# FFN up products on x times norm weight with the root applied behind, five tall sets in each FFN, and one pool of weight tiles for the whole kernel

## The chip, the cores and the metric

The kernel runs on one core of a Trainium2 chip. The metric is the device time of one execution in microseconds (us). Before the change the median of three runs is 1173.68 us (1173.27 to 1174.42). The engines are TensorE (PE: matmuls; PEld: its weight loads), VectorE (DVE), ScalarE (ACT), GpSimd (POOL) and SyncE (SP). Each takes its instructions strictly in the order in which they stand in its own queue. SP and POOL also issue DMA transfers.

## The reference

One block of a language model in float32, with 512 tokens and model width 1024: an FFN, a mixer (a short convolution and a gated linear attention) and a second FFN, each on a normalised input and each added to the residual.

```python
def rmsnorm(x, g):
    y = x * lax.rsqrt(jnp.mean(x * x, axis=-1, keepdims=True) + EPS)
    return y * g
def swiglu(x, w_gu, w_down):
    g, u = jnp.split(x @ w_gu, 2, axis=-1)          # w_gu: 1024 x 5632
    return (jax.nn.silu(g) * u) @ w_down            # w_down: 2816 x 1024
...
x = x + 0.5 * swiglu(rmsnorm(x, norm_ffn1_g), ffn1_w_gu, ffn1_w_down)
x = x + hybrid_mixer(rmsnorm(x, norm_mix_g), w_in, ...)
x = x + 0.5 * swiglu(rmsnorm(x, norm_ffn2_g), ffn2_w_gu, ffn2_w_down)
return rmsnorm(x, final_norm_g)
```

## The kernel before

**Tiles.** x lies transposed: eight tiles `x[k]` of 128 features by 512 tokens. Every float32 product is made of three matmuls in the reduced type fp32r: each operand is split in a high part (a cast) and a low part (the rest), and the product is high times high, high times low, low times high. A weight tile `f` of 128x1024 (512 KB) comes by a DMA on SP's queue; ScalarE casts it into `wh` (line 393) and VectorE subtracts that into `wl` (394). There are three buffers of `wh` and three of `wl`, so a step's cast waits until TensorE has finished the step three before it; the method `take` of the class `Weights` issues the split of a step two steps ahead.

**Three ways of multiplying.** *Plain*: `mm_group` and `mm_single` multiply one 128-column block of weights at a time, with the weights as the stationary operand and x's 512 tokens moving: 24 matmuls of 512 columns for one block of 128 outputs. *Tall* (`Tall.run`) and *set* (`Set.run`) use a Strassen-like scheme: seven products, named m1, p2, q6, p5, q7, p3 and p4, in place of eight. A tall covers four blocks of gate columns and four of up columns with 168 matmuls of 512 columns, has x as the stationary operand, and so gives its result with the tokens on the partitions; `turn` transposes it back (32 transposes of 128x128 for a tall). A set covers two blocks of each with 168 matmuls of 256 columns, with no transposes. The seven operands made of x (class `Operands`, tiles `op`, lines 676 and 677) are sums of quarters of the normalised x, kept in the last eight tiles of `hid`; those made of the weights are sums that POOL makes with adding DMAs (line 362) and VectorE.

**The FFN's up products before.** The 22 pairs of blocks are four plain (two in `mm_group`, which is started while x still comes in, and two in `mm_single`), four talls and one set. The plain ones use `Norm`: x times the norm weight, split as it is (lines 496 to 500), and the root of the mean square as a row `row` that multiplies the outputs on VectorE (`plain_pair`). The sum of squares over the features is two matmuls with a matrix of ones (529, 530). The talls and the set use x times norm weight times row (`normed`, line 757).

**Order.** TensorE's order in the talls and sets is program order (`manual_schedule`); elsewhere a scheduler sets the order of each engine when the kernel is built, and the chip keeps to it. The pools of `hid`, `tp` and `f` belong to a phase (first FFN, mixer, second FFN) and are opened anew in each.

Of the kernel before, what the change touches and what calls it, by code (L numbers as in the profile page):

```python
# [103 lines left out]
PLAIN1, PLAIN2 = 4, 4  # L104
# [27 lines left out]
TALL_ORDER = ("m1", "p2", "q6", "p5", "q7", "p3", "p4")  # L132
TALL = {}


def tall(name, mat, cols, base=0):
# [6 lines left out]
    STEPS.extend((n, p) for p in TALL_ORDER for n in firsts)  # L143

# [13 lines left out]
def up_plan(up, plain, slow):  # L158

    kinds = ["tall"] * ((KF - plain) // 4)  # L160
    kinds.insert(len(kinds) if slow else 1, "set")
    f = plain
    for kind in kinds:
        if kind == "tall":
            tall((up, f), up, (f * P, DFF + f * P))
# [11 lines left out]
def ffn_plan(up, down, plain, slow):  # L177

    units(group(up, KD, (0, DFF, P, DFF + P), slow))
    for f in range(2, plain):  # L180
        units(single(up, KD, f * P))
        units(single(up, KD, DFF + f * P))
    up_plan(up, plain, slow)
# [32 lines left out]
ffn_plan("ffn1_w_gu", "ffn1_w_down", PLAIN1, True)  # L216
mixer_plan()
ffn_plan("ffn2_w_gu", "ffn2_w_down", PLAIN2, False)
# [8 lines left out]
def block_kernel(ctx: ExitStack, tc: tile.TileContext, xT, vecs, gf, gup, wgl, wts, out):  # L227
# [76 lines left out]
    for n, b in (("wh", 3), ("wl", 3), ("op", 14)):  # L304
        pools[n] = ctx.enter_context(tc.tile_pool(name=n, bufs=b))
    acc_row = ctx.enter_context(tc.tile_pool(name="acc_row", bufs=1))
    class Weights:
# [15 lines left out]
        def phase(self, early, first=6):  # L323
# [4 lines left out]
            for i in range(lo, self.end):  # L328
                n, p = STEPS[i]
                if p == "m1" and n in TALL:  # L330
                    self.loads.setdefault(i - (4, 3)[TALL[n][1]], []).append(n)
                    self.firsts.setdefault(i - (1, 0)[TALL[n][1]], []).append(n)
# [31 lines left out]
        def issue(self):  # L364
            at = self.issued
            self.fetch(at)
            for n in self.loads.get(at, ()):
                self.raw[n] = [self.dma(n + i) for i in range(4)]
# [144 lines left out]

    def rstd_rows(accs, width):
# [47 lines left out]
    class Set:  # L562
# [8 lines left out]

        def run(self, p):
            b = {"m1": "b", "p2": "a", "q6": "b", "p5": "c", "q7": "b", "p4": "b", "p3": "c"}[p]
            if self.group.joint:
                return self.run_joint(p, b)
# [6 lines left out]
            for k in range(4):  # L582
                for e in range(2):
                    s = slice(k * HW + e * P, k * HW + (e + 1) * P)
                    t = slice(k * HW, (k + 1) * HW)
                    to = o[:, e * HW : (e + 1) * HW]
                    for j, (ww, aa) in enumerate(((h, bh), (h, bl), (l, bh))):
# [9 lines left out]
        def run_joint(self, p, b):  # L597
            fresh = b not in self.bank
            two_banks = b != "b"
            if fresh:  # L600
                self.bank[b] = MM2() if two_banks else MM()
            o = self.bank[b]
            parts = self.group.get(p)
            h, l = W.take()
            for k in range(4):
                a = parts[k // 2][:, (k % 2) * S : (k % 2 + 1) * S]
                for e in range(2):
                    s = slice(k * HW + e * P, k * HW + (e + 1) * P)
                    if two_banks:
                        nc.tensor.matmul(o[:, e], h[:, s], a, start=fresh and k == 0,  # L610
                                         stop=False, skip_group_check=True)
                        nc.tensor.matmul(o[:, e, HW:], l[:, s], a[:, :HW], start=False,
                                         stop=k == 3, skip_group_check=True)
                        continue
                    to = o[:, e * HW : (e + 1) * HW]
                    for j, (ww, aa) in enumerate(((h, a[:, :HW]), (h, a[:, HW:]),
                                                  (l, a[:, :HW]))):
                        nc.tensor.matmul(to, ww[:, s], aa, start=fresh and k == 0 and e == 0 and j == 0,
                                         stop=k == 3 and j == 2, skip_group_check=True)
            if p in self.keep:  # L620
                v = T()
                nc.scalar.copy(v, o)
                self.v[p] = v
            self.done(self, p)

    class Operands:
# [5 lines left out]
        def __init__(self, b, joint=False):  # L632
            self.b = b
            self.joint = joint
            self.parts = {}
            self.sums = set()
# [20 lines left out]
        def make(self, p):  # L657
            if p in self.parts:
                return
            i = self.ORDER.index(p)  # L660
            if i > 0:
                self.make(self.ORDER[i - 1])
            v = self.sum(p)
            if self.joint:
                t = [tile_of("op", [P, 1024], F32R) for _ in range(2)]
                for i in range(2):
                    a = t[i].rearrange("p (k b t) -> p k b t", b=2, t=HW)
                    vi = v[:, 2 * i : 2 * i + 2]
                    nc.scalar.copy(a[:, :, 0], vi)
                    nc.vector.tensor_tensor(out=a[:, :, 1], in0=vi,  # L670
                                            in1=a[:, :, 0].bitcast(F32), op=ALU.subtract)
                self.parts[p] = t
                return
# [61 lines left out]
    def ffn(up, down, norm, nxt, plain, at):  # L735
        xh, xl = norm.h, norm.l
        rows = []

        def finish(k):
            if k == at:  # L740
                rows.append(norm.finish())

        o = mm_group(up, KD, (0, DFF, P, DFF + P), xh, xl, extra=finish, slow=nxt is not None)
        row = rows[0]
        hid = tile_of("hid", [P, KF, S])
        xn = {}

        def normed(j, l):


            if (j, l) not in xn:
                t = slice(l * HW, (l + 1) * HW)
                f = KF - KD + 4 * j
                v = hid[:, f : f + 4, t]
                for i in range(4):
                    k = 4 * j + i
                    nc.vector.scalar_tensor_tensor(
                        out=v[:, i], in0=x[k][:, t],
                        scalar=vec[:, norm.goff + k : norm.goff + k + 1], in1=row[:, t],
                        op0=ALU.mult, op1=ALU.mult)  # L760
                xn[j, l] = v
            return xn[j, l]

        xo = Operands(normed)

        def plain_pair(f, g, u):
            s, t = T(), T()
            mul(s, g, row)
            nc.scalar.activation(s, s, AF.Silu)
            mul(t, u, row)  # L770
            mul(hid[:, f], s, t)

        xo.make("m1")
        plain_pair(0, o[0], o[1])
        xo.make("p2")
        plain_pair(1, o[2], o[3])
        for f in range(2, plain):
            g = mm_single(up, KD, f * P, xh, xl)
            u = mm_single(up, KD, DFF + f * P, xh, xl)
            if f == 2:  # L780
                xo.make("p5")
            if f == 3:
                xo.sum("q6")
            plain_pair(f, g, u)
# [3 lines left out]
        def up_tall(f):  # L788
            g, u = {}, {}

            def done(p, banks):
                for t in range(2):
# [16 lines left out]
                    if p == "p3":  # L809
                        nc.vector.tensor_tensor(out=g[2 + t], in0=b, in1=g[2 + t], op=ALU.add)  # L810
                        nc.scalar.activation(g[2 + t], g[2 + t], AF.Silu)
                        mul(u[t], u[t], g[2 + t])
                    if p == "p4":
                        nc.vector.scalar_tensor_tensor(out=g[t], in0=b, scalar=-1.0, in1=g[t],
                                                       op0=ALU.mult, op1=ALU.mult)
# [13 lines left out]

        def up_set(i):  # L830
            f = [f for kind, f in UPS[up] if kind == "set"][i]
            h = hid[:, f : f + 2]

            def done(s, p):
                bank, v = s.bank, s.v
                if p == "p2":
                    s.g1 = T()
                    nc.vector.tensor_tensor(out=s.g1, in0=bank["a"], in1=v["m1"], op=ALU.add)
                    nc.scalar.activation(s.g1, s.g1, AF.Silu)
# [4 lines left out]
                if p == "p4":  # L844
                    nc.vector.scalar_tensor_tensor(
                        out=h[:, :, :HW], in0=pair(bank["b"]), scalar=-1.0, in1=pair(s.g1),
                        op0=ALU.mult, op1=ALU.mult)
                if p == "p3":
                    g2 = T()
                    nc.vector.tensor_tensor(out=g2, in0=bank["c"], in1=v["q6"], op=ALU.add)  # L850
                    nc.scalar.activation(g2, g2, AF.Silu)
                    mul(h[:, :, HW:], pair(s.u2), pair(g2))

            return Set(xo, done)
# [35 lines left out]
        def begin(i):  # L890
            kind, f = UPS[up][i]
            return [((up, f), 1, "m1"), ((up, f), 0, "p2")] if kind == "tall" else \
                [(0, "q6"), (0, "p5")]

        count = 0
        for i, (kind, f) in enumerate(UPS[up]):
            if kind == "set":
                continue
            keys = (begin(i + 1) if i + 1 < len(UPS[up]) else
                    [((down, 0), 1, "m1"), ((down, 0), 0, "p2")])  # L900
# [797 lines left out]
```

## Time and profile before

| | |
|---|---|
| median of three runs | 1173.68 us |
| the profiled execution's own time | 1173.56 us |
| its span (first to last instruction) | 1171.8 us |
| TensorE busy | 1161.5 us, 99% of the span |
| VectorE, ScalarE, POOL busy | 899.6, 643.0, 121.6 us |
| first FFN's plain products | 5.68 to 50.11 us |
| first FFN's set (mixed with the last tall's end) | 202.35 to 229.93 us |
| second FFN's plain products | 828.69 to 872.70 us |
| last matmul | 1165.02 us |

A span is the time between the first and the last instruction of one execution; the execution's own time holds some 1.8 us more around it. Matmuls overlap: one takes 390 ns, but they begin every 227 ns or so, and it is the distance between beginnings that adds up. ScalarE's and VectorE's instructions overlap by about 0.1 us in the same way. In a timeline's row the first number is the start, the second the time to the end of the last of the xN instructions.

### The profile page before, as it was taken

The page shows a single profiled execution, that of the slowest core. Times are in us where ns is not written, and L with a number is a line of the kernel's source. Part 1 is how long each engine was busy: PE and PEld are TensorE (multiplying, and loading weights), DVE is VectorE, ACT ScalarE, POOL GpSimd, SP SyncE. Part 2 cuts the span into 40 slices and gives each one's busy share as a digit, 9 for nine tenths or more (in the row PEclk, how much of TensorE's full clock was granted, in tenths as well). Part 3 has the DMA queues.
Part 4 walks back from the last instruction along what each step waited for, and adds up shares of the span by engine and source line. Part 5 has one row for each costly group of instructions (what it writes and reads, how often), then busy time and mean ns, then how long its engine had stood idle before and what let it go on. Part 6 is the DMA issues. An engine that isn't in the chain of part 4 may idle for free.

```text
span 1171.8 us, 16449 instructions
## 1 busy us (share of the span) xinstructions
PE 1161.5 (99%) x6410; PEld 1012.3 (86%) x6410; DVE 899.6 (77%) x1081; ACT 643.0 (55%) x811; POOL 121.6 (10%) x161
## 2 busy tenths in 40 slices
PE   9999999999999999999999999999999999999997
PEld 8888888999988888789999998888888988888886
DVE  7985657879887976777797999556598566699965
ACT  6555555635452757474654577524356555575543
POOL 0101110011110110111010112000010111101100
PEclk9999999999999999999999999999999999999999
DMA  9667785647485485877566788811746777867711
GB/s 362 132 187 170 173 221 154 170 121 180 104 283 144 93 219 155 201 206 208 141 162 158 176 201 220 288 36 50 247 112 158 195 191 155 205 177 171 179 49 72
DMA packets 59006, 200.07 MB, mean 171 GB/s; under 512 B 6865, under 2 KB 6993, under 8 KB 58929
## 3 DMA queue, kind: packets, MB, share of 16 engines
q0 software_dynamic: 19424, 70.26, 31.7%
q1 hardware_dynamic: 36912, 124.27, 31.5%
q10 hardware_dynamic: 2592, 4.49, 1.0%
q8 instruction: 50, 0.82, 0.3%
q14 instruction: 28, 0.22, 0.1%
HBM read 124.55 MB, written 8.39 MB: 113 GB/s over the span
## 4 chain that ended last, share of the span: by engine, by line
PE 96%; DVE 2%; ACT 1%; issue 1%; DMA 0%; POOL 0%; DVEq 0%; ACTq 0%; POOLq 0%
PE mm L704 44%; PE mm L588 22%; PE mm L445 7%; PE mm L422 3%; PE mm L423 3%; PE mm L421 3%; PE mm L464 1%; PE mm L463 1%; PE mm L462 1%; PE aux L826 1%; PE mm L1020 1%; PE mm L1018 1%; PE mm L1019 1%; DVE wl L394 1%; PE aux L1320 1%
## 5 line engine op out<-in xcount | busy, mean ns | idle before, releaser
L393 ACT CAST wh<-f 128x1024 fp32r<-128x1024 f32 (+1 forms) x343 | 359.2, 1048 | 381.2 <-PE mm L704 120.3
L394 DVE TENSOR_TENSOR wl<-f,wh 128x1024 fp32r<-128x1024 f32 (+1 forms) x343 | 416.8, 1218 | 184.9 <-ACT wh L393 180.1
L704 PE MATMUL mm<-wh,op 128*128 128x512 f32 x1568 | 492.4, 391 | 0.0
L704 PEld LDWEIGHTS mm<-wh,op 128*128 128x128 f32 x1568 | 294.4, 188 | 60.4
L704 PE MATMUL mm<-wl,op 128*128 128x512 f32 x784 | 305.7, 390 | 0.7 <-DVE wl L394 0.7
L588 PE MATMUL mm<-op,wh 128*128 128x256 f32 x1568 | 284.6, 284 | 0.6 <-ACT tp L593 0.6
L588 PEld LDWEIGHTS mm<-op,wh 128*128 128x128 f32 x1568 | 245.0, 192 | 1.7 <-ACT tp L593 0.8
L588 PE MATMUL mm<-op,wl 128*128 128x256 f32 x784 | 222.2, 283 | 1.1 <-DVE wl L394 1.1
L362 POOL DMA_DIRECT2D f<-f x126 | 108.6, 863 | 919.4 <-DVE wl L394 336.4
L704 PEld LDWEIGHTS mm<-wl,op 128*128 128x128 f32 x784 | 147.3, 188 | 31.2 <-DVE wl L394 1.5
L588 PEld LDWEIGHTS mm<-op,wl 128*128 128x128 f32 x784 | 150.3, 192 | 1.6 <-DVE wl L394 1.5
L445 PE MATMUL mm<-op,wh 128*128 128x512 f32 x256 | 64.0, 391 | 0.0
L421 PE MATMUL mm<-op,wh 128*128 128x512 f32 x164 | 63.8, 389 | 0.0
L422 PE MATMUL mm<-op,wh 128*128 128x512 f32 x164 | 63.8, 389 | 0.0
L423 PE MATMUL mm<-op,wl 128*128 128x512 f32 x164 | 63.8, 389 | 0.0
L445 PEld LDWEIGHTS mm<-op,wh 128*128 128x128 f32 x256 | 48.0, 188 | 10.3 <-issue 0.2
L676 ACT CAST op<-hid 128x1024 fp32r<-128x1024 f32 x42 | 43.9, 1048 | 18.7 <-PE mm L704 12.7
L677 DVE TENSOR_TENSOR op<-hid,op 128x1024 fp32r<-128x1024 f32 x42 | 51.2, 1220 | 3.6 <-ACT op L676 3.4
L387 DVE TENSOR_TENSOR f<-f,f 128x1024 f32<-128x1024 f32 x28 | 34.2, 1221 | 5.6 <-DMA f<-f 4.6
L421 PEld LDWEIGHTS mm<-op,wh 128*128 128x128 f32 x164 | 30.8, 188 | 6.5
L422 PEld LDWEIGHTS mm<-op,wh 128*128 128x128 f32 x164 | 30.8, 188 | 6.4
L423 PEld LDWEIGHTS mm<-op,wl 128*128 128x128 f32 x164 | 30.8, 188 | 6.3
(283 smaller groups left out, 1146.0 us busy)
## 6 DMA issues: line engine op xcount, KB each, us to landing
f<-wts SPq DMA_DIRECT2D x219, 512.0 KB, 4.3
f<-f POOLq DMA_DIRECT2D x126, 512.0 KB, 5.0
X<-xT SPq DMA_DIRECT2D x8, 256.0 KB, 5.3
xs<-X POOLq DMA_DIRECT2D x8, 256.0 KB, 6.3
ga<-tp ACTq DMA_DIRECT2D x8, 256.0 KB, 4.9
gb<-tp ACTq DMA_DIRECT2D x8, 256.0 KB, 3.8
tp<-ga SPq DMA_DIRECT2D x8, 256.0 KB, 4.8
X<-xs POOLq DMA_DIRECT2D x8, 256.0 KB, 7.4
```

The lines of the kernel that those rows point to most:

```text
L362: nc.gpsimd.dma_start(out_, a, accum_op=ALU.add)
L387: nc.vector.tensor_tensor(out=a11, in0=a11, in1=a22, op=ALU.subtract)
L393: nc.scalar.copy(h[:, :w], raw[:, :w])
L394: nc.vector.tensor_tensor(out=l[:, :w], in0=raw[:, :w], in1=h[:, :w].bitcast(F32), op=ALU.subtract)
L421: nc.tensor.matmul(o, wh, ah, start=first, stop=False)
L422: nc.tensor.matmul(o, wh, al, start=False, stop=False)
L423: nc.tensor.matmul(o, wl, ah, start=False, stop=last)
L445: nc.tensor.matmul(o[c], w[:, s : s + P], a[k], start=k == 0 and j == 0, stop=k == kt - 1 and j == 2)
L588: nc.tensor.matmul(to, ww[:, s], aa[:, t], start=fresh and k == 0 and e == 0 and j == 0, stop=k == 3 and j == 2, skip_group_check=True)
L676: nc.scalar.copy(hv, v)
L677: nc.vector.tensor_tensor(out=lv, in0=v, in1=hv.bitcast(F32), op=ALU.subtract)
L704: nc.tensor.matmul(self.bank[b][e], aa[:, c], ww, start=fresh and i == 0 and n == 0, stop=k == 3 and n == 2, skip_group_check=True)
```

## The change

1. The second norm class `Gain` leaves the root out of every operand of the FFNs' up products. The operands are made of x times norm weight alone, and the root, now a column of one number per token (`norm.r`, and `norm.minus` for its negative), is a scale of the Silu on ScalarE and of VectorE's product behind the matmuls. The sum of squares is four matmuls of one column, in place of the two with a matrix of ones; the row, its transposes and `plain_pair` go.
2. First FFN: two plain blocks instead of four, five talls and no set. The plain ones (`start`) have x as stationary operand, in blocks that are at once the operands m1, p2 and p3 of the talls (`parts`), and the four column blocks of weights moving: 96 matmuls of 512 columns as before, in program order on TensorE. `turn_pair` transposes the result (8 transposes).
3. Second FFN: no plain blocks, five talls and one set. The set (`Turned`) exchanges stationary and moving operands, so that the root is a column there too, and its result is transposed (8 transposes).
4. x times norm weight is written to the last eight tiles of `hid` by eight activations on ScalarE at the head of `ffn` (line 773 of the new kernel); before, VectorE did this in 16 instructions of 256 columns, times the row. In the first FFN the gained halves that are split are 256 columns wide.
5. The order of the seven products differs in the first tall of each FFN and the last of the second; the weights of the first tall of each FFN may be asked for sooner.
6. The pool `f` is opened once for the whole kernel. Its tiles are loaded for the next phase as soon as buffers come free.
7. In the first FFN the last tall's transposes stand between the first plain down products, and the two of these that need the same banks come behind them.

The core of the diff:

```diff
-PLAIN1, PLAIN2 = 4, 4
+FIRST1 = ("m1", "p2", "p5", "q6", "q7", "p3", "p4")
+FIRST2 = ("m1", "p5", "p2", "q6", "q7", "p3", "p4")
...
-    kinds = ["tall"] * ((KF - plain) // 4)
-    kinds.insert(len(kinds) if slow else 1, "set")
+    kinds = ["tall"] * ((KF - first) // 4)
+    if first == 0:
+        kinds.insert(1, "set")
...
-    for n, b in (("wh", 3), ("wl", 3), ("op", 14)):
+    for n, b in (("wh", 3), ("wl", 3), ("op", 14), ("f", 10)):
...
+    class Gain:
+        def add(self, k, sooner=False):
+            ...
+                ls = (0, 1) if j else (1, 0)
+            ...
+                for l in ls:
+                    h, w = (t[:, i * HW : (i + 1) * HW] for t in self.parts[j, l])
+                    v = x[k][:, l * HW : (l + 1) * HW]
+                    if sooner and k == 0:
+                        nc.vector.tensor_scalar(out=h, in0=v, scalar1=g, scalar2=None,
+                                                op0=ALU.mult)
+                    else:
+                        nc.scalar.activation(h, v, AF.Copy, scale=g)
+                    nc.vector.scalar_tensor_tensor(out=w, in0=v, scalar=g, in1=h.bitcast(F32),
+                                                   op0=ALU.mult, op1=ALU.subtract)
+            ...
+        def finish(self):
+            st = AUX()
+            for t in range(NTB):
+                nc.tensor.matmul(st[:, t : t + 1], self.acc[:, t * P : (t + 1) * P],
+                                 ones[:, 0:1], start=True, stop=True)
+            ...
-    def ffn(up, down, norm, nxt, plain, at):
+    def ffn(up, down, hid, norm, nxt):
+        XN = KF - KD
+        for k in range(KD):
+            nc.scalar.activation(hid[:, XN + k], x[k], AF.Copy, scale=norm.g(k))
...
+            def start(u):
+                h, l = W.take(u)
+                for i in range(u[2]):
+                    ...
+                    for t in range(NTB):
+                        ...
+                        nc.tensor.matmul(o[t], a, wh, start=k == 0, stop=False)
+                        nc.tensor.matmul(o[t], a, wl, start=False, stop=False)
+                        nc.tensor.matmul(o[t], b, wh, start=False, stop=k == KD - 1)
+                    if k == KD - 2:
+                        norm.finish()
...
-                        nc.scalar.activation(g[t], g[t], AF.Silu)
+                        nc.scalar.activation(g[t], g[t], AF.Silu, scale=norm.r[t])
...
-                        nc.vector.scalar_tensor_tensor(out=g[t], in0=b, scalar=-1.0, in1=g[t],
-                                                       op0=ALU.mult, op1=ALU.mult)
+                        nc.vector.scalar_tensor_tensor(out=g[t], in0=b, scalar=norm.minus[t],
+                                                       in1=g[t], op0=ALU.mult, op1=ALU.mult)
...
-    FFN = dict(f=10, hid=1, tp=9)
+    FFN = dict(hid=1, tp=9)
```

What this does to the order on the engines at three places follows. `wh` and `f` are the weights' tiles, `op` the split operands of x, `acc` and `tp` the sum of squares and its parts.

ScalarE at the start of the first FFN, before: behind the last of x's eight parts comes the cast of the plain group's fourth weight tile.

```order
L499 ACTIVATE op_178<-X,vec 128x512
L508 ACTIVATE tp_182<-X 128x512
L499 ACTIVATE op_178<-X,vec 128x512
L508 ACTIVATE tp_187<-X 128x512
L393 CAST wh_216<-f_206 128x1024
L393 CAST wh_234<-f_208 128x1024
```

The same place now.

```order
L555 ACTIVATE op_175<-X,vec 128x256
L555 ACTIVATE op_177<-X,vec 128x256
L562 ACTIVATE tp_204<-X 128x512
L773 ACTIVATE hid_119<-X,vec 128x512 x7
L408 CAST wh_253<-f_233 128x1024
L408 CAST wh_270<-f_235 128x1024
L408 CAST wh_298<-f_237 128x1024
L711 CAST op_437<-hid_119 128x1024
```

Each gained part is two instructions of half the width, and seven of the eight copies to `hid` stand between x's last part and the cast `wh_253` of the fourth weight tile.

VectorE at the same place now (before, the row behind the last `acc` was the fourth tile's `wl`):

```order
L563 TENSOR_TENSOR acc_144<-acc_144,tp_204 128x512
L691 TENSOR_TENSOR hid_119<-hid_119 128x4x256
L696 TENSOR_TENSOR hid_119<-hid_119 128x4x256
L409 TENSOR_TENSOR wl_254<-f_233,wh_253 128x1024
L409 TENSOR_TENSOR wl_271<-f_235,wh_270 128x1024
```

Two sums of quarters (for p5 and q7), which read the copies in `hid`, now stand ahead of the fourth tile's `wl_254`.

SP's queue at the end of the first FFN, before: the two weights `wgl` and `gup` of the mixer's gate are asked for ahead of the mixer's weight tiles.

```order
L358 DMA f_2885<-wts 128x1024
L358 DMA f_3006<-wts 128x1024
L1140 DMA tp_3244<-wgl 128x128
L1153 DMA tp_3256<-gup 16x512 x6
L358 DMA f_3205<-wts 128x1024
L358 DMA f_3207<-wts 128x1024
```

The same place now; the first two rows are the first FFN's last two weight tiles, and `f_3140` is the mixer's first.

```order
L367 DMA f_2824<-wts 128x1024
L367 DMA f_2945<-wts 128x1024
L367 DMA f_3140<-wts 128x1024
L367 DMA f_3142<-wts 128x1024
L367 DMA f_3144<-wts 128x1024
L367 DMA f_3146<-wts 128x1024
L367 DMA f_3209<-wts 128x1024
L367 DMA f_3215<-wts 128x1024
L367 DMA f_3249<-wts 128x1024
L367 DMA f_3283<-wts 128x1024
L367 DMA f_3285<-wts 128x1024
L367 DMA f_3287<-wts 128x1024
```

Twelve weight tiles of the mixer (the ten in the rows above, and `f_3289` and `f_3291` behind them) now stand ahead of `wgl`; the last, `f_3291`, takes the buffer of `f_3142` and so waits for the mixer's second `wl`.

On VectorE at the mixer's start the third and the fourth `wl` of the mixer's group and a split of `acc` now stand ahead of the eight small instructions that make the gate's weights `g` of `wgl`; before, `g` came ahead of the fourth `wl` and of that split.

More of the change, by code (lines that the diff above doesn't have):

```diff
@@ L174, with ffn_plan @@
 UPS = {}
[L177 to L183, printed above, removed]
+UP_ORDER = {}
+GU = (0, P, DFF, DFF + P)
+def ffn_plan(up, down, slow):
+    if slow:
+        units(group(up, KD, GU, True))
+    up_plan(up, 2 if slow else 0)
     if slow:
@@ L595, in run, with products, __init__ @@
             self.done(self, p)
[L597 to L624, printed above, removed]
+    class Turned(Set):
+        def products(self, bh, bl, h, l):
+            return (bh, h), (bh, l), (bl, h)
     class Operands:
         ORDER = ("m1", "p2", "p5", "q6", "q7", "p3", "p4")
-        def __init__(self, b, joint=False):
+        def __init__(self, b, order_=ORDER, parts=()):
             self.b = b
-            self.joint = joint
-            self.parts = {}
+            self.order = order_
+            self.parts = dict(parts)
             self.sums = set()
@@ L659, in make @@
                 return
-            i = self.ORDER.index(p)
+            i = self.order.index(p)
             if i > 0:
-                self.make(self.ORDER[i - 1])
+                self.make(self.order[i - 1])
             v = self.sum(p)
[L664 to L673, printed above, removed]
             h, l = (tile_of("op", [P, 1024], F32R) for _ in range(2))
```

218 lines of the change are left out of this document (138 added, 80 removed).

## The prediction

> **What bounds the kernel now.** I read the page first.
>
> ```profile
> span 1171.8 us, 16449 instructions
> ...
> PE 1161.5 (99%) x6410; PEld 1012.3 (86%) x6410; DVE 899.6 (77%) x1081; ACT 643.0 (55%) x811; POOL 121.6 (10%) x161
> ...
> PEclk9999999999999999999999999999999999999999
> ...
> PE 96%; DVE 2%; ACT 1%; issue 1%; DMA 0%; POOL 0%; DVEq 0%; ACTq 0%; POOLq 0%
> ```
>
> TensorE is busy for 99% of the span at its full clock, and 96% of the chain that ended last is its own work. So the time is TensorE's instructions plus every pause they are given. The two stages that the change rewrites hold no pause to win, as the windows over the plain products of the first FFN and of the second show (columns: window, length, then busy us and instructions of PE, PEld, DVE, ACT, POOL, the clock, the DMA share, GB/s):
>
> ```profile
> 5.68:27.95 22.27, 22.27 (x98) 18.43 (x98) 20.00 (x33) 15.68 (x24) 1.01 (x1) 1.00 1.02 400
> 828.69:850.91 22.22, 22.22 (x99) 18.36 (x99) 11.41 (x20) 8.12 (x10) 1.00 (x2) 1.00 0.56 168
> 850.91:872.70 21.79, 21.79 (x98) 18.05 (x97) 20.90 (x33) 9.70 (x12) 2.48 (x3) 1.00 0.43 104
> ```
>
> PE is busy for all of each. In the first one VectorE is busy for 20.0 of 22.3 us and ScalarE for 15.7: work added there has little room.
>
> **TensorE's work.** The chain gives the distance between beginnings (start, time, engine, line, count):
>
> ```profile
> 50.11 43.52 PE mm L704 x192
> 93.63 0.87 PE aux L826 x8
> 251.48 80.63 PE mm L588 x672
> 443.51 0.45 PE aux L1320 x4
> ```
>
> A matmul of 512 columns is worth 43.52/192 = 0.2267 us, one of 256 columns 80.63/672 = 0.120, a transpose 0.87/8 = 0.109. Counting both orders: matmuls of 512 columns go from 3618 to 3662 (the four with a matrix of ones go, each FFN gets 24 more of the rest), of 256 columns from 2364 to 2196 (the first FFN's set), transposes from 286 to 334. So +44 x 0.2267 = +10.0, -168 x 0.120 = -20.2, +48 x 0.109 = +5.2. The eight float32 matmuls of one column are in no trace; a float32 matmul shows as two records, so 16: at the 0.113 of L1320's float32 records of 128 columns that is 1.8 (upper end), at a quarter of it 0.4 (lower). I take the middle of the two, about 0.9, since a single column streams next to nothing but still loads its weights. Sum **-4.1** (-4.6 to -3.2). Moving the root from operands to Silu scales and products keeps ScalarE's and VectorE's counts there, so it costs nothing while they trail TensorE; VectorE's rows fall from 1082 to 1051.
>
> **The start of the first FFN.** This is the timeline of the three engines before (start, time to the end, engine, line, operation, tiles, count):
>
> ```profile
> 1.11 4.64 PE L292 MATMUL aux<-ones 128*128 128x128 f32 x20 [1.11 <-POOL ones L289]
> 5.68 2.22 PE L445 MATMUL mm<-op,wh 128*128 128x512 f32 x8
> 16.81 1.98 PE L445 MATMUL mm<-op,wh 128*128 128x512 f32 x8
> 4.52 0.63 ACT L505 ACTIVATE acc<-X 128x512 f32<-128x512 f32 x1
> 13.88 0.70 ACT L499 ACTIVATE op<-X,vec 128x512 fp32r<-128x512 f32 x1
> 14.49 0.62 ACT L508 ACTIVATE tp<-X 128x512 f32<-128x512 f32 x1
> 15.01 1.98 ACT L393 CAST wh<-f 128x1024 fp32r<-128x1024 f32 x2
> 5.06 0.48 DVE L496 TENSOR_SCALAR op<-X,vec 128x512 fp32r<-128x512 f32 x1
> 5.57 1.41 DVE L500 SCALAR_TENSOR_TENSOR op<-X,vec,op 128x512 fp32r<-128x512 f32 x2
> 16.83 3.49 DVE L394 TENSOR_TENSOR wl<-f,wh 128x1024 fp32r<-128x1024 f32 x3
> ```
>
> ScalarE works without a break from 4.52 to 15.01 and then casts the fourth weight tile (k = 4 and 5), 1.8 us before TensorE comes to it at 16.81. That slack is all there is. By form, with the mean of one behind the busy time:
>
> ```profile
> L499 ACT ACTIVATE op<-X,vec 128x512 fp32r<-128x512 f32 x23 | 16.4, 714 | 9.9 <-DVE X L941 6.8 <-DVE X L1624 3.0
> L508 ACT ACTIVATE tp<-X 128x512 f32<-128x512 f32 x21 | 13.0, 617 | 0.0
> L1292 ACT COPY g<-aux 128x384 f32<-128x384 f32 x4 | 1.9, 480 | 2.9 <-PE aux L1291 2.9
> L1304 ACT COPY g<-aux 128x256 f32<-128x256 f32 x4 | 1.5, 368 | 0.0
> ```
>
> A gain of 512 columns takes 0.71 and the next begins 0.61 later (13.88 to 14.49). 128 columns are 0.11 (480 less 368 ns), so half the width is 0.49 to 0.51, begun 0.41 apart. Now 14 halves stand where 7 gains stood: 14 x 0.41 - 7 x 0.61 = +1.5. All eight copies to `hid` (gains of 512 columns) stand ahead of the cast too, seven right in front of it: 8 x 0.61 = +4.9. The fourth cast starts at 15.0 + 1.5 + 4.9 = 21.4, less 0.2 for a step that overlaps, so 21.2, and ends at 22.2. On VectorE the two sums of quarters that follow the copies take some 1.14 each (the distance in the row of three `wl`: (3.49 - 1.22)/2, with 1.22 for the last) and hold `wl` to 22.45, ended 23.7.
>
> TensorE begins about 0.45 later: VectorE makes four operands of half the width ahead of the first matmul, in place of one of 0.48 whose successor TensorE didn't wait for. With a wait of 0.4 for the third tile, whose cast comes 0.9 later, it has finished that tile at 5.68 + 0.45 + 48 x 0.2267 + 0.4 = 17.4. It then stands until 22.2, does one matmul (the second already reads `wl`), and stands until 23.7: a pause of 6.0 us. The 47 matmuls left and the four sums of squares (0.9) end at 23.7 + 10.7 + 0.9 = 35.25, against 27.95 before. Less the 0.45 by which this stretch's own work grew (0.9 for the 0.45 of L529 and L530), already counted above, that is **+6.85** (bounds: +4.65 if copies and halves come 0.1 us closer together, which takes 2.2 off the queue; +9.2 with the clock, below). What comes behind keeps up: the next casts and `wl` run back to back at 1.1 each from 23.7, TensorE takes 5.4 for each tile.
>
> **The mixer's start.** The weights of the gate come by one small transfer, are split in eight small VectorE instructions, and feed eight matmuls in the midst of the mixer's group:
>
> ```profile
> tp<-wgl SPq DMA_DIRECT2D x1, 64.0 KB, 3.3
> ...
> 347.31 1.22 DVE L394 TENSOR_TENSOR wl<-f,wh 128x1024 fp32r<-128x1024 f32 x1
> 350.98 1.22 DVE L394 TENSOR_TENSOR wl<-f,wh 128x1024 fp32r<-128x1024 f32 x1
> 352.11 0.30 DVE L1146 CAST g<-tp 128x64 fp32r<-128x64 f32 x2
> ...
> 353.15 0.36 DVE L1147 TENSOR_TENSOR g<-tp,g 128x64 fp32r<-128x64 f32 x2
> 353.43 0.63 DVE L1150 CAST g<-g 128x128 fp32r<-128x128 f32 x4
> ...
> 353.97 0.40 PE L1165 MATMUL aux<-op,g 128*96 128x512 f32 x1
> ```
>
> TensorE asked for `g` at 353.97 and VectorE had just made it. Now `wgl` is requested behind a tile that waits for the second `wl` (ended 348.5): asked for at 349.0, landed at 352.3, by 3.3 us. VectorE turns to `g` later than that: after the third `wl` (352.1) come the fourth (1.14) and a split of `acc` (0.6), so the small ones begin at 353.85 and, with 1.2 to the first use, `g` is there at 355.0. **+1.0**; from 0, if the eight matmuls move on, to +3, if `wgl` lands 2 us later behind twelve tiles of 512 KB. I take the order's own sum.
>
> **The second FFN's start.** The first tall stands where plain products stood. It needs only parts of x that exist, and weights now come sooner through the common pool. VectorE is the tightest there (20.90 of 21.79 in the third window): I reach 854.1 for a `wl` that TensorE wants at 854.0. 0 (to +1). The copies to `hid` there are eight of 0.61 on a ScalarE that is busy for 8.1 of 22.2 us, so they are hidden; if they weren't, rival D holds it. The new orders of the seven products, the transposes set between the first down products and the `turn` of the set cost nothing beyond their instructions, since TensorE has products of the other half to do meanwhile (a tall's product is 24 matmuls, 5.4 us); without that cover each would show the trip through ScalarE's copy of a bank and back, some 0.6 us. The down products and the tail stay.
>
> Sum: -4.1 + 6.85 + 1.0 = **+3.75**. The profiled execution took 1173.56, 0.12 under the median: 1173.56 + 3.75 = **1177.3 us**.
>
> **Rivals.** Less than 0.2%, 2.35 us, can't be told from no change here.
>
> *A, the pause costs the clock.* How long TensorE may rest at full clock is seen at the end only. The last matmul, and the clock in the third column from the right:
>
> ```profile
> 1164.62 0.39 PE L1020 MATMUL mm<-op,op 128*128 128x512 f32 x1
> 1168.00:1169.00 1.00, 0.00 (x0) 0.00 (x0) 0.17 (x1) 0.41 (x1) 0.00 (x0) 1.00 0.00 0
> 1169.00:1170.00 1.00, 0.00 (x0) 0.00 (x0) 0.00 (x0) 0.00 (x0) 0.00 (x0) 0.97 0.97 367
> 1170.00:1171.00 1.00, 0.00 (x0) 0.00 (x0) 0.00 (x0) 0.00 (x0) 0.00 (x0) 0.50 0.40 158
> ```
>
> It halved near 1169.94, 4.9 us after the end at 1165.0. My first pause is 4.8, a hair less, and a second of 1.3 follows one matmul. If the clock falls, the return costs what the opening shows: 20 matmuls of 128 columns in 4.64, 0.232 each against 0.113 later, so half of 4.64, 2.3 us: **1179.6**. The Trainium skill's page "TensorE: Matmul & The Clock Gate", Part 1 on the HAM clock gate, speaks against this change: the clock falls to half after about one idle window of 3.4 us, and needs as much sustained work to return. By that rule an estimate of 1.7 us would be added. The trace's one long rest had 4.9 us at full clock, longer than the page's figure.
>
> *B, faster: ScalarE gets past its copies in time.* Then only -4.1 + 0.85 (late begin, third tile) remain, with the mixer covered: **1170.3**. For it speaks that TensorE's work does fall. It decides if the fourth `wl` ends by about 18.7 rather than 23.7, so that the pause is under 1 us; that takes ScalarE some 5 us less than its rows say, hence little.
>
> *C, no change: the queue is shorter.* Copies 0.1 us and halves 0.1 us closer, -0.8 and -1.4: **1175.1**.
>
> *D, further pauses.* Where the fourth tile's delay hands VectorE a backlog in the second FFN's first tall (+1) and `wgl` lands 2 us late (+2): **1180.3**.
>
> **Chances.** Forecast (1176.0 to 1178.8) 0.44, A 0.15, B 0.11, C 0.16, D 0.14. Faster is B, 0.11; same is C, 0.16; slower the rest, 0.73. The range leaves out B and the far ends of A and D: 1174.4 to 1181.0.
>
> **What would show it.** Seven rows of copies to `hid` ahead of ScalarE's cast; TensorE idle from about 17.4 to 22.2 and, after one matmul, to 23.7, ended by `wl`; the clock between 22 and 28 full (A: half); the plain group ended at about 35.3; the gate's first matmul in the mixer waiting some 1 us for `g`; no gap behind the second FFN's first matmul. It fails if TensorE's busy time doesn't fall by about 4 us, or if the fourth cast stands clear of the copies.

## The result, and the profile after

The changed kernel took **1181.25 us** (median of 4 runs, 1179.98 to 1182.0); the kernel before, on the same chip, 1173.74. The ratio is 1.0062 (95% interval 1.0045 to 1.0080): 7.5 us slower. Forecast were 3.7 us slower and a range up to 1181.0. The sign came out, the size was half of what came, and the median lies 0.25 us above the range.

The page of the changed kernel (its profiled execution took 1179.98, the fastest of the four):

```profile
span 1178.3 us, 16386 instructions
...
PE 1162.9 (99%) x6350; PEld 1008.0 (86%) x6350; DVE 888.6 (75%) x1050; ACT 669.3 (57%) x855; POOL 130.2 (11%) x170
...
PEclk8999999999999999999999999999999999999999
...
PE 93%; DVE 2%; ACT 2%; DMA 2%; issue 1%; SPq 0%; DVEq 0%; ACTq 0%
```

TensorE is busy for as long as before (1162.9 for 1161.5 us), though it has less to do, and the first slice of its clock is an 8. The low clock comes from the first plain group. Its timeline, ScalarE, VectorE, then TensorE:

```profile
16.67 4.39 ACT L773 ACTIVATE hid<-X,vec 128x512 f32<-128x512 f32 x7
20.96 2.93 ACT L408 CAST wh<-f 128x1024 fp32r<-128x1024 f32 x3
21.09 1.22 DVE L696 TENSOR_TENSOR hid<-hid 128x1024 f32<-128x1024 f32 x1 [1.23 <-ACT hid L773]
22.23 3.49 DVE L409 TENSOR_TENSOR wl<-f,wh 128x1024 fp32r<-128x1024 f32 x3
17.41 0.39 PE L796 MATMUL mm<-wh,op 128*128 128x512 f32 x1
22.05 0.79 PE L794 MATMUL mm<-wh,op 128*128 128x512 f32 x1 [4.25 <-ACT wh L408]
23.50 0.79 PE L795 MATMUL mm<-wl,op 128*128 128x512 f32 x1 [0.67 <-DVE wl L409]
24.52 0.63 PE L794 MATMUL mm<-wh,op 128*128 128x512 f32 x1
27.56 0.39 PE L796 MATMUL mm<-wh,op 128*128 128x512 f32 x1
```

Seven copies to `hid`, then the cast of the fourth weight tile at 20.96; TensorE ends the third tile's last matmul at 17.8, does one at 22.05, and goes on at 23.50. The matmuls from there on take 0.63 and begin 0.43 apart, where they take 0.39 and begin 0.23 apart from 27.1 on. The windows of that stretch (the third column from the right is the granted clock) show why:

```profile
16.86:20.27 3.41, 0.94 (x5) 0.44 (x3) 2.76 (x5) 3.41 (x6) 0.00 (x0) 1.00 1.02 408
20.27:23.68 3.41, 0.97 (x2) 0.46 (x3) 2.59 (x3) 3.41 (x5) 0.00 (x0) 0.50 0.95 378
23.68:27.10 3.42, 3.42 (x9) 2.65 (x10) 3.39 (x4) 1.15 (x2) 1.88 (x2) 0.50 0.85 178
27.10:30.51 3.41, 3.41 (x16) 2.81 (x15) 3.38 (x4) 2.01 (x2) 0.00 (x0) 1.00 0.90 241
```

The clock was half for exactly two windows of 3.41 us, 20.27 to 27.10.

By stages, from the beginnings of TensorE's matmuls (us):

| | first matmul | first FFN | mixer | second FFN | last matmul |
|---|---|---|---|---|---|
| before | 5.68 | 337.2 | 485.7 | 336.1 | 1164.6 |
| changed | 6.22 | 344.9 | 485.4 | 334.5 | 1171.05 |
| difference | +0.54 | +7.8 | -0.3 | -1.6 | +6.4 |

(The second FFN's first matmul before begins at 828.52; the 828.69 in the table ahead of the change is the end of the matmul in front of it.) Nearly all of the loss is in the first FFN; the second gains 1.6.

### The profile page after: what moved, and what is told of

Its sections match the earlier page's. It is cut to its first block, busy times and chain, and to the rows that moved or that the text cites. A ratio compares the mean times of both kernels' runs of the same rounds, so it can differ in the third digit from the quotient of the medians.

```text
span 1178.3 us, 16386 instructions
## 1 busy us (share of the span) xinstructions
PE 1162.9 (99%) x6350; PEld 1008.0 (86%) x6350; DVE 888.6 (75%) x1050; ACT 669.3 (57%) x855; POOL 130.2 (11%) x170
## 4 chain that ended last, share of the span: by engine, by line
PE 93%; DVE 2%; ACT 2%; DMA 2%; issue 1%; SPq 0%; DVEq 0%; ACTq 0%
PE mm L739 50%; PE mm L657 20%; PE mm L460 4%; PE mm L436 2%; PE mm L437 2%; PE mm L438 2%; PE aux L853 1%; PE mm L479 1%; PE mm L478 1%; PE mm L477 1%; DMA f<-f 1%; DVE wl L409 1%; PE mm L1084 1%; PE mm L1082 1%; PE mm L1083 1%
## 5 line engine op out<-in xcount | busy, mean ns | idle before, releaser
L739 PE MATMUL mm<-wh,op 128*128 128x512 f32 x1792 | 564.1, 392 | 0.0
L739 PEld LDWEIGHTS mm<-wh,op 128*128 128x128 f32 x1792 | 336.5, 188 | 70.6 <-ACT tp L831 1.3
L739 PE MATMUL mm<-wl,op 128*128 128x512 f32 x896 | 349.3, 390 | 0.6 <-DVE wl L409 0.6
L657 PE MATMUL mm<-op,wh 128*128 128x256 f32 x1344 | 243.6, 284 | 0.1
L657 PEld LDWEIGHTS mm<-op,wh 128*128 128x128 f32 x1344 | 209.9, 192 | 0.9 <-ACT tp L662 0.3
L657 PE MATMUL mm<-op,wl 128*128 128x256 f32 x672 | 190.5, 284 | 1.1 <-DVE wl L409 1.1
L657 PEld LDWEIGHTS mm<-op,wl 128*128 128x128 f32 x672 | 128.8, 192 | 1.6 <-DVE wl L409 1.5
L436 PE MATMUL mm<-op,wh 128*128 128x512 f32 x100 | 39.1, 391 | 0.0
L438 PE MATMUL mm<-op,wl 128*128 128x512 f32 x100 | 38.9, 389 | 0.0
L437 PE MATMUL mm<-op,wh 128*128 128x512 f32 x100 | 38.9, 389 | 0.0
L460 PE MATMUL mm<-op,wh 128*128 128x512 f32 x128 | 32.1, 391 | 0.0
L460 PEld LDWEIGHTS mm<-op,wh 128*128 128x128 f32 x128 | 23.9, 188 | 5.1
L855 ACT COPY hid<-aux 128x512 f32<-128x512 f32 x40 | 21.5, 592 | 6.4 <-PE aux L853 6.4
L477 PE MATMUL mm<-wh,op 128*128 128x512 f32 x64 | 25.1, 392 | 0.0
L479 PE MATMUL mm<-wh,op 128*128 128x512 f32 x64 | 24.9, 390 | 0.0
```

Source lines behind the costliest of these rows:

```text
L436: nc.tensor.matmul(o, wh, ah, start=first, stop=False)
L437: nc.tensor.matmul(o, wh, al, start=False, stop=False)
L438: nc.tensor.matmul(o, wl, ah, start=False, stop=last)
L460: nc.tensor.matmul(o[c], w[:, s : s + P], a[k], start=k == 0 and j == 0, stop=k == kt - 1 and j == 2)
L657: nc.tensor.matmul(to, ww[:, s], aa[:, t], start=fresh and k == 0 and e == 0 and j == 0, stop=k == 3 and j == 2, skip_group_check=True)
L739: nc.tensor.matmul(self.bank[b][e], aa[:, c], ww, start=fresh and i == 0 and n == 0, stop=k == 3 and n == 2, skip_group_check=True)
```

## The experiments

Each run is compared with the kernel before on the same chip (medians 1174.3 to 1174.5 there).

**Copies behind the group.**

```diff
-        for k in range(KD):
-            nc.scalar.activation(hid[:, XN + k], x[k], AF.Copy, scale=norm.g(k))
...
                 for u in group(up, KD, GU, True):
                     start(u)
+            copies()
```

> The changed kernel with the first FFN's copies to hid written behind the plain group, so that seven of them stand behind the fourth, fifth and sixth casts of weights on ScalarE. Theory (the seven copies make the pause, and the pause halves the clock): the fourth cast starts near 16.7 us in place of 20.96, TensorE's pauses fall from 6.0 to about 2.0 us, the clock stays full; 4.0 + 2.2 us gone, so 1181.25 - 6.2 = about 1175. Rival (the pause is the weights' or x's arrival, and what stands behind is late anyway): the group ends within 1 us of where it did, 1180 or more. Rival (copies only, clock not tied to the pause): 4 us, 1177.

Measured: 1175.05 (11 runs), ratio 1.0007 (0.9999 to 1.0016). ScalarE and TensorE's longest wait in this kernel:

```profile
16.57 2.93 ACT L408 CAST wh<-f 128x1024 fp32r<-128x1024 f32 x3
19.40 4.41 ACT L774 ACTIVATE hid<-X,vec 128x512 f32<-128x512 f32 x7
...
PE mm L799 <- DVE wl L409: 1.3, 1, 1.3
```

The cast starts 4.4 us sooner, the pause is 1.6, the clock stays full, and the time is 6.2 us under the changed kernel's, by the medians. So the queue of copies ahead of the fourth cast is the cause of most of the loss, through the pause and what hangs on it.

**Ten matmuls in the pause.**

```diff
-                for u in group(up, KD, GU, True):
+                for i, u in enumerate(group(up, KD, GU, True)):
+                    if i == 3:
+                        for _ in range(WARM):
+                            nc.tensor.matmul(warm[:, :P], ones, ones, start=True, stop=True)
                     start(u)
```

(`WARM` is 10.)

> The changed kernel with ten float32 matmuls of 128 columns on the matrix of ones (20 records, some 2.3 us, results unused) on TensorE between the third and the fourth weight tile of the first plain group. The pause for the cast stays, but TensorE rests in it for 2.1 us only. Theory (the clock falls because of the rest's length): first matmul of the fourth tile still at 22.05, the next 20 at 0.23 us apart and not 0.43; about 2.2 us less, 1179. Rival (the low clock comes from something else, such as the opening): no gain, 1181.

Measured: 1181.16, ratio 1.0052 (1.0040 to 1.0065). The expectation failed: no gain that can be told. Its windows, cut where the clock changes:

```profile
17.58:20.99 3.41, 2.50 (x22) 2.27 (x20) 1.93 (x4) 3.41 (x7) 0.00 (x0) 1.00 1.01 405
20.99:24.40 3.41, 1.59 (x6) 1.10 (x7) 3.41 (x4) 3.41 (x4) 0.00 (x0) 1.00 0.84 324
24.40:27.82 3.42, 3.42 (x10) 2.64 (x9) 3.39 (x3) 0.25 (x1) 1.88 (x2) 0.50 0.96 279
```

The longest rest is 1.8 us now, yet the clock fell again, for one window, and when TensorE was at work again. Here it isn't the longest rest that decides but how much of a window TensorE was busy: 2.50 of 3.41 kept the clock, 1.59 lost it. And the window in which it is then halved was all work, so one window cost about as much as the two with the pause in them (the first FFN takes 344.8 us, 344.9 in the changed kernel).

**Squares behind too.**

```diff
+            if self.parts is None or k < 3:
+                self.square(k)
...
                     start(u)
+                    if i == 2:
+                        for k in range(3, KD):
+                            norm.square(k)
+            copies()
```

> As the one with the copies behind the group, and the squares of x's parts 3 to 7 with their sums written behind the third tile's matmuls too. Theory: ScalarE reaches the fourth cast near 14.6 us, its wl is ready near 17, and TensorE's pause there is gone; what is left of the change is 3.2 us less TensorE work, a start 0.5 later, 0.3 at the third tile: about 1172, below the kernel before (1173.7). Rival (the change has another cost behind the start that the pause hides): 1174 to 1176.

Measured: 1180.14, ratio 1.0052 (1.0038 to 1.0065). The rival was right in kind, and the time lies 4 us beyond what it said. The pause at the fourth tile is gone, but a new one stands behind the group, where the plain pair is transposed; VectorE's first and last small instruction of the root, ScalarE's Silu, and TensorE:

```profile
26.88 0.16 DVE L577 TENSOR_SCALAR col<-aux 128x4 f32<-128x4 f32 x1
35.92 0.16 DVE L580 TENSOR_SCALAR col<-col 128x4 f32<-128x4 f32 x1
37.60 1.57 ACT L818 ACTIVATE tp<-mm,col 128x256 f32<-128x256 f32 x4
38.74 2.10 PE L875 MATMUL aux<-ident,tp 128*128 128x128 f32 x8 [3.58 <-DVE tp L819]
```

Seven instructions of 0.16 us need 9 us, since each stands between sums and splits of 1.2 us. The changed kernel has the same chain of the root, from 34.2 to 36.6 us there: its pause let VectorE be done with the sums before, so that only one split stands within the chain. Here too a half clock (from 40.20) follows: its window before was busy for 1.33 us.

**The pool opened anew in each phase.**

```diff
-    for n, b in (("wh", 3), ("wl", 3), ("op", 14), ("f", 10)):
+    for n, b in (("wh", 3), ("wl", 3), ("op", 14)):
...
-    FFN = dict(hid=1, tp=9)
+    FFN = dict(hid=1, tp=9, f=10)
```

(and `f=10` for the mixer's phase)

> The changed kernel with the weights' pool f opened anew in each phase as before (ten buffers each). Theory (the common pool moves loads that were in time anyway): within 1 us of the changed kernel's 1181.25. Rival (the common pool brings the mixer's or the second FFN's first weights in time): 1 to 4 us slower. Rival (the common pool costs, by the gate's weights asked for late): up to 1 us faster.

Measured: 1202.89, ratio 1.0242 (1.0228 to 1.0256): 21.6 us slower than the changed kernel, far beyond the rival's 1 to 4. At the second FFN's start, SP's queue, ScalarE and TensorE:

```profile
840.66 8.07 SPq L367 DMA_DIRECT2D f<-wts  x9
844.60 0.71 ACT L773 ACTIVATE hid<-X,vec 128x512 f32<-128x512 f32 x1
847.61 1.04 ACT L408 CAST wh<-f 128x1024 fp32r<-128x1024 f32 x1
848.70 0.80 PE L739 MATMUL mm<-wh,op 128*128 128x512 f32 x1 [5.40 <-ACT wh L408]
```

The phase's first weights are asked for only at 840.66, 2.3 us ahead of the mixer's last matmul (842.91). Their first cast comes behind the last copy to `hid` and two casts of `op`, TensorE waits 5.4 us for it, and further waits and windows at half clock follow (clock half from 845.94 to 856.18, and in three other places). Against the changed kernel's stages the first FFN takes 5.0 us more, the mixer 7.1 and the second FFN 10.0.

**The pool alone, in the kernel before** (the same lines the other way round).

> The kernel before with one part of the change alone: the weights' pool f is opened once for the whole kernel. Theory (the common pool is worth its 21 us only where a phase begins with talls, whose products want four weight tiles and their sums at once; the kernel before begins its second FFN with plain products that need one tile in 5.4 us, and has no pause there): within 0.2% of the kernel before, 1174.3. Rival (the pool is a gain of its own): 2 us or more faster. Rival (it costs, since the gate's weights in the mixer are asked for behind more tiles): 1 to 2 us slower.

Measured: 1173.65, ratio 0.9996 (0.9987 to 1.0005), the theory's case. The common pool does nothing that can be told for the old order, and the new one needs it.

**Both pauses filled.**

```diff
+                        if k == 4 and t == 0:
+                            for _ in range(18):
+                                nc.tensor.matmul(warm[:, :P], ones, ones, start=True, stop=True)
                         nc.tensor.matmul(o[t], a, wh, start=k == 0, stop=False)
+                        if k == 4 and t == 0:
+                            for _ in range(5):
+                                nc.tensor.matmul(warm[:, :P], ones, ones, start=True, stop=True)
                         nc.tensor.matmul(o[t], a, wl, start=False, stop=False)
```

> The changed kernel with float32 matmuls of 128 columns on ones (results unused) in both of TensorE's pauses: 18 (36 records, 4.1 us) ahead of the fourth tile's first matmul and 5 (10 records, 1.1 us) ahead of its second. The waits for the cast and for wl stay where they were. The windows of 3.41 us in which the clock was granted so far fell to half after a window with TensorE busy for 1.6 us or less (28% to 46%) and stayed full after 1.6 us or more (47% up). Theory (the clock's share is the time that TensorE rests within a window): no window below half, the clock stays full from 6 us to the end, the group ends 2.2 us sooner than in the changed kernel's profile; 1181.25 - 2.2 to 3 = 1178.2 to 1179. Rival (the clock's share is small, as the ten matmuls of the earlier trial brought 0.1 us): 1181.

Measured: 1179.65, ratio 1.0044 (1.0032 to 1.0057).

```profile
22.06 0.50 PE L797 MATMUL mm<-wh,op 128*128 128x512 f32 x1 [0.25 <-ACT wh L408]
23.52 0.50 PE L801 MATMUL mm<-wl,op 128*128 128x512 f32 x1
...
20.27:23.68 3.41, 3.16 (x26) 2.89 (x26) 2.58 (x3) 3.41 (x5) 0.00 (x0) 1.00 0.95 375
23.68:27.10 3.42, 3.42 (x16) 2.81 (x17) 3.39 (x4) 1.18 (x2) 1.88 (x2) 1.00 0.82 231
```

The two matmuls wait until the same moments as in the changed kernel, the clock is full until the tail, and the first FFN is 343.3 us against 344.9. From the second of these matmuls to the tenth behind it, 2.39 us pass here and 4.06 in the changed kernel. So the clock's share is 1.6 to 1.7 us; the intervals of the two ratios overlap, so the medians (1.6 us apart) alone wouldn't show it, but the clock and the stage do.

**The root in one piece.**

Against the kernel with the squares behind, the order on two more engines is program order here, and the plain pair's Silu and products stand inside:

```diff
-            with tc.manual_schedule(engines={ENG.PE}):
+            with tc.manual_schedule(engines={ENG.PE, ENG.DVE, ENG.Activation}):
...
+                    if i == 3:
+                        copies(range(KD - 1))
...
+                copies((KD - 1,))
```

> As the one with squares and copies behind (1180.1, where TensorE waited 3.6 us at 38.7 us for the plain pair scaled by the root), with ScalarE's and VectorE's order in the group written by hand so that the small instructions that make the root follow one another, Silu and products of the pair come right behind, and the eighth copy to hid only then. Theory (the wait was VectorE's six small instructions between sums and splits of 1.2 us each, from 26.9 to 36.1): root ready near 29, pair near 32, no wait at the transposes, clock full; 1174.4 (the kernel before on this chip) - 3.2 of TensorE's work + 0.5 at the start + 0.3 at the third tile + 0.8 of small gaps in the second FFN - 0.5 in the mixer = about 1172.3. Rival (a further wait behind it, for the operands of p5 whose copies are later now): 1175 or more.

Measured: 1173.60 (11 runs), ratio 0.9999 (0.9990 to 1.0008). The root's first and last step and the Silu:

```profile
26.73 0.16 DVE L577 TENSOR_SCALAR col<-aux 128x4 f32<-128x4 f32 x1 [0.66 <-PE aux L573]
28.94 0.17 DVE L580 TENSOR_SCALAR col<-col 128x4 f32<-128x4 f32 x1
31.99 1.57 ACT L819 ACTIVATE tp<-mm,col 128x256 f32<-128x256 f32 x4
```

2.2 us in place of 9, and no wait at the transposes. All 7.5 us are recovered, but the 2 us beyond that were not to be had: first FFN 337.3, mixer 485.8, second FFN 334.5.

**The first operand first.**

```diff
-                ls = (0, 1) if j else (1, 0)
+                ls = (0, 1)
```

> As the one before, with the halves of x's first four parts made in the order 0, 1 in place of 1, 0, so that the half which the first matmul reads is made first. Theory (the late first matmul is this order): first matmul near 5.7 us in place of 6.1 to 6.2, about 0.4 us less, 1171.9. Rival (the second half, needed six matmuls later, is then late by as much): no difference.

Measured: 1173.36 (11 runs), ratio 0.9991 (0.9983 to 1.0000).

```profile
5.44 0.47 PE L802 MATMUL mm<-wh,op 128*128 128x512 f32 x1
12.01 0.50 PE L803 MATMUL mm<-wl,op 128*128 128x512 f32 x1 [0.65 <-DVE wl L409]
9.65 1.05 ACT L408 CAST wh<-f 128x1024 fp32r<-128x1024 f32 x1 [0.46 <-DMA f<-wts]
```

Against the kernel with the root in one piece, the first matmul is 0.9 sooner (6.32 to 5.44), and 0.65 of it is given back at the third tile, whose weights come only then by DMA. This has the lowest median of all: level with the kernel before, or at most 0.2% faster.

**The changed kernel once more.**

> The changed kernel once more, unaltered, for a second profile of it. Theory (the windows of 3.41 us in which the clock is granted stand anywhere against the pause, which itself is the same each time): TensorE's pauses again 4.6 us from beginning to beginning and 1.4, the clock half for one or two whole windows, but from another moment on; time 1180 to 1182. Rival (the clock falls a fixed time after the last matmul): half from 20.3 us again.

Measured: 1181.37, ratio 1.0058 (1.0041 to 1.0075).

```profile
15.11:18.53 3.42, 2.90 (x13) 2.06 (x11) 3.42 (x8) 3.42 (x8) 0.00 (x0) 1.00 1.03 410
18.53:21.94 3.41, 0.00 (x0) 0.00 (x0) 1.94 (x3) 3.41 (x6) 0.00 (x0) 1.00 1.02 408
21.94:25.36 3.42, 2.41 (x5) 1.62 (x6) 3.42 (x4) 3.13 (x4) 1.01 (x1) 0.50 0.67 220
25.36:28.77 3.41, 3.41 (x10) 2.64 (x9) 3.34 (x4) 0.39 (x1) 0.86 (x1) 0.50 0.93 286
```

The same pauses, but the clock is half from 21.94 to 28.77, not from 20.27. The windows lie anywhere against the work; here more work falls into the half ones, and the first FFN is 345.7, not 344.9.

## Why the prediction was wrong

The sum, term by term, with what the first profile holds in its place (us):

| term | forecast | found |
|---|---|---|
| TensorE's work | -4.1 | -1.5 |
| late begin and pauses of the first FFN | +6.85 | +6.5 |
| the clock | 0 | +1.7 |
| the mixer | +1.0 | -0.3 |
| sum | +3.75 | +6.4 |

The work is the two FFNs of the kernel with the root in one piece less those of the kernel before (its longest wait for `wl` is 0.6 us, 0.7 in the kernel before). The second row is what the changed kernel's first FFN takes more than that kernel's (344.9 for 337.3), less the clock's share, and the late begin.

- **Two steps failed.** The larger is the term of TensorE's work, mis-sized by 2.6 us (below). The other is the threshold by which the clock was put at nothing, in rival A: "My first pause is 4.8, a hair less" than the 4.9 us after which the clock fell at the tail. The tail's 4.9 was read as the rest that TensorE is allowed. It was one window of 3.41 without work (1166.53 to 1169.94) and what was left of the window before. By the windows listed at the end, a pause as long as the forecast's spoils one wherever the windows lie: halved between two of them, 4.8 us leave 1.0 us of work in each. The clock fell 2.5 us after the last matmul's end. Rival A had this mechanism, at a chance of 0.15 and a price of 2.3, where 1.7 was found. That its time, 1179.6, lies so near the profiled 1179.98 is luck: the work was 2.6 us too low in it, the mixer 1.3 too high.
- **The page of the Trainium skill** that A cites ("TensorE: Matmul & The Clock Gate", Part 1) speaks of a window of about 3.4 us that runs by itself. Every stretch of half clock ahead of the tail is 3.41, 6.83 or 10.24 us long and begins at any time against the work, so the traces agree; the prediction set the page against the tail's 4.9 us, and the two did not contradict each other. By its "after ≥1 idle window", though, a window with 0.94 or 1.59 us of work would have kept the clock, and here it did not. The 1.7 us that the prediction estimated by it is what the clock cost.
- **The pause** came as forecast: cast at 20.96 (21.2), first matmul 22.05 (22.2), the second 23.50 (23.7), start +0.54 (+0.45), about 0.2 at the third tile (0.4). The mechanism of this term was right, and moving the copies showed it.
- **TensorE's work**, by distances between beginnings over both FFNs, from the kernel before to the one with the root in one piece: matmuls of 256 columns -20.3 (forecast -20.2), transposes +4.8 (+5.2), the 16 records of one column 0.10 each, +1.6 (+0.9), matmuls of 512 columns +12.4 (+10.0). The last is the main error: 0.2267 us was read within products and taken for all. Behind each group of transposes the next matmul waits 0.09 longer, and first matmuls on new operands 0.1 to 0.3. In the new FFNs 40 distances lie more than 0.05 us above 0.2267, by 4.2 us in all; in the kernel before there are 21, by 2.0 us. That is 2.2 of the 2.4 us. Why a matmul behind transposes comes late stays open. TensorE's busy time, which was to fall by about 4 us, rose by 1.4 at the low clock and falls by 1.6 with the root in one piece. So the first FFN's new plan, even without the long pauses, is worth nothing (337.3 for 337.2 us), and only the second gains.
- **The mixer** did not lose its 1.0 us:

```profile
358.40 2.35 DVE L409 TENSOR_TENSOR wl<-f,wh 128x1024 fp32r<-128x1024 f32 x2
360.68 0.68 DVE L488 TENSOR_TENSOR tp<-acc,tp 128x512 fp32r<-128x512 f32 x1
361.28 0.29 DVE L1210 CAST g<-tp 128x64 fp32r<-128x64 f32 x2
362.26 0.39 PE L1229 MATMUL aux<-op,g 128*96 128x512 f32 x1
```

The order is the one that was read, but the third `wl` begins 7.2 us after the mixer's first matmul (351.16) and not 8.1 as before (350.98 less 342.86), and the gate's matmul came without a wait, 11.1 us after the mixer's first as before. The forecast took VectorE's place in time from the old trace; the last additions to x now end a microsecond earlier against TensorE.
- **The second FFN** has no wait at its start, as forecast, and the common pool is the reason: the sentence on it was right, but what hangs on it, 10.0 us there and 21.6 in all, was not priced.
- **What is left** of 7.5: the first profile explains 6.4. The other runs are up to 2 us longer, and most of that stays open. The second profile of the same kernel has 0.7 of it in the first FFN, by the clock's windows. The mixer, too, takes from 485.4 to 487.6 us in the profiles (485.7 in the kernel before; 492.5 with a pool for each phase, left out here). In the kernel with the copies behind the group (487.6) ScalarE stands before a transfer of the mixer for 5.5 us, where its longest such wait in the kernel before is 3.9:

```profile
739.48 0.63 ACT L1647 ACTIVATE tp<-tp 128x512 f32<-128x512 f32 x1 [5.51 <-DMA tp<-ga]
```

- A slip in the part on the kernel before: a tall has 16 transposes, not 32 (128 of line 826 for the eight talls). The counts of the prediction (286 to 334) came from the instructions and hold.

## What to carry to other kernels

Where an engine works without a break up to the moment at which its result is wanted, every instruction set ahead of that moment, once the slack is used up, lengthens a pause of TensorE. Here the sum over the queue gave the pause's ends to within 0.3 us: do the queue's sum for anything moved to the start of a stage, and put what is wanted later behind what is wanted now. Add to a pause of TensorE the clock that goes with it: not by the length of the rest, but by how much work a window of 3.4 us, wherever it lies, may be left with. Price instructions where they stand, too: a distance read within one long product was too short for matmuls that come behind transposes or on new operands. And a pause hides what stands behind it: with this one taken away, a chain of seven small instructions was stretched to 9 us by the work set between them, and TensorE waited for it.

## What the runs showed of the hardware

In these runs TensorE's clock changes at the ends of windows of 3.41 us that begin at any time against the program. After a window the clock went to half where TensorE had been busy for 0, 0.49, 0.71, 0.78, 0.89, 0.94, 1.33 or 1.59 us of it (busy time by the profile), and stayed full at 1.52, 1.60, 1.78, 1.90, 2.10 and 2.50. So the limit lies between 39% and 47% of the window. The 1.59 that lost the clock and the 1.52 that kept it are out of order, so the profile's busy time isn't quite what is counted, and these figures tell the limit no closer. In the kernel with a pool for each phase, for example, and last the window at the end of the kernel with both pauses filled, from 1169.57, which kept the clock:

```profile
16.50:19.91 3.41, 1.60 (x8) 0.98 (x6) 3.16 (x6) 3.41 (x7) 0.00 (x0) 1.00 1.03 410
19.91:23.33 3.42, 0.49 (x1) 0.19 (x1) 2.20 (x3) 3.42 (x6) 0.00 (x0) 1.00 1.03 411
23.33:26.74 3.41, 2.91 (x7) 2.33 (x8) 3.41 (x4) 1.83 (x2) 1.88 (x2) 0.50 0.61 179
1169.57:1172.98 3.41, 1.52 (x7) 0.94 (x5) 2.30 (x7) 1.93 (x6) 0.00 (x0) 1.00 0.41 154
```

The window from 19.91 still had full clock, the next one half. At half clock a window with 2.41 us of work did not bring the full clock back (the changed kernel's second profile), windows with 2.89 and 2.91 did. As an estimate from these figures, a pause of some 2.5 us costs a window at half clock, up to 1.7 us, where it falls into one window, and nothing where it is shared evenly between two that are otherwise full of work.
